# Grouped-query attention on one core: part of the exponentials as linear pieces on VectorE, row tiles one head apart, and a planned instruction order

## The chip, the cores and the metric

One core of a Trainium2 chip. The metric is device time in microseconds (us) of one execution. Executions come with a state: a run more than 1.5% above the fastest of the same kernel counts as slow, and only fast runs are compared.

## The reference

Batch 8, 8 query heads, 2 key/value heads, 1024 positions, 64 columns per head, all float32. Cut to what matters:

```python
q, k, v = (np.random.randn(8, n, 1024, 64).astype(np.float32) * 0.1 for n in (8, 2, 2))

for g in range(n_kv_heads):                       # 2 groups of 4 query heads
    scores = scale * np.matmul(q_group, k_group.transpose(0, 1, 3, 2))   # scale = 1/8
    attn = np.exp(scores - scores.max(axis=-1, keepdims=True))
    attn = attn / (attn.sum(axis=-1, keepdims=True) + 1e-08)
    output[:, q_start:q_end] = np.matmul(attn, v_group)
```

With these inputs a score has a standard deviation of about 0.01 (64 products of size 0.01, times 1/8), so every weight is within a few per cent of every other.

## The kernel before

A *cell* is one score block: 128 keys x 512 queries of one head. There are 1024 of them. Head 0 of a pair lives in the upper 64 rows of TensorE (row tile 0), head 1 in the lower 64 (row tile 1). ScalarE takes the exp of three cells at once (1536 columns):

```python
nc.tensor.matmul(                                  # L125: one score cell
    state["tile"][:, len(state["cells"]), :],
    lhsT=kT[b][side * D : (side + 1) * D, c * 128 : (c + 1) * 128],
    rhs=qT[(b, j)][side * D : (side + 1) * D, qb * QBS : (qb + 1) * QBS],
    start=True, stop=True)
...
nc.scalar.activation(out=pt[:, 0 : len(cells), :],  # L105
    in_=state["tile"][:, 0 : len(cells), :], func=AF.Exp, scale=scale)
```

The output product of a cell is eight small matmuls, four blocks of 128 queries times two halves of the 128 keys; each half uses one row tile and 65 columns of `v` (the last column is ones and gives the sum). Both row tiles add into the same output bank, one after the other, and a no-op on the Sync queue, the *turn*, hands the bank over:

```python
mm = nc.tensor.matmul(                              # L148
    ops[:, side, qs * (D + 1) : (qs + 1) * (D + 1)],
    lhsT=pcell[(u * NKC + c, side)][lo : lo + 64, qs * 128 : (qs + 1) * 128],
    rhs=vt[(b, side)][lo : lo + 64, c, :], ...)
...
turn[0] = nc.sync.nop().ins                         # L162
tc.add_manual_dep(turn[0], last.ins.name, SYNC, reason="bank")
```

The same Sync queue carries the DMA transposes that bring `q` and `k` in, forty of them, each of all 1024 rows:

```python
nc.gpsimd.dma_start(out=qscr..., in_=q[b, j::NPAIR]...)   # cast to 16 bit through DRAM
nc.sync.dma_start_transpose(out=qt, in_=qscr)             # L81
```

The softmax here doesn't subtract the row's maximum and nothing guards it: scores larger than these inputs give would overflow.

Of the kernel before, what the change touches and what calls it, by code (L numbers as in the profile page):

```python
# [7 lines left out]


@with_exitstack  # L10
def kernel(
    ctx: ExitStack,
    tc: tile.TileContext,
    q: bass.AP,
    k: bass.AP,
    v: bass.AP,
    out: bass.AP,
):
    nc = tc.nc
    FP32 = mybir.dt.float32  # L20
    BF16 = mybir.dt.bfloat16
    AF = mybir.ActivationFunctionType
    ALU = mybir.AluOpType

    B, H, S, D = q.shape
    G = k.shape[1]
    NPAIR = H // G
    NKC = S // 128
    QBS = 512
    NQB = S // QBS  # L30
    NQS = QBS // 128
    scale = 1.0 / math.sqrt(D)




    units = [(b, j, qb) for b in range(B) for j in range(NPAIR) for qb in range(NQB)]
    NSTEP = len(units) * NKC
    LAG = NKC + 2
    WIDTHS = (3, 3)  # L40

    scr_pool = ctx.enter_context(
        tc.tile_pool(name="scr", bufs=2, space=bass.MemoryType.DRAM)
    )
    qT_pool = ctx.enter_context(tc.tile_pool(name="qTpool", bufs=2 * NPAIR))
    kT_pool = ctx.enter_context(tc.tile_pool(name="kTpool", bufs=2))
    v_pool = ctx.enter_context(tc.tile_pool(name="vpool", bufs=3 * G))
    p_pool = ctx.enter_context(tc.tile_pool(name="ppool", bufs=12))
    ostage_pool = ctx.enter_context(tc.tile_pool(name="ostage", bufs=3))
    recip_pool = ctx.enter_context(tc.tile_pool(name="recip", bufs=3))  # L50
    spools = [
        ctx.enter_context(
            tc.tile_pool(name=f"spsum{w}", bufs=1, space=bass.MemoryType.PSUM)
        )
        for w in range(len(WIDTHS))
    ]
    opool = ctx.enter_context(
        tc.tile_pool(name="opsum", bufs=1, space=bass.MemoryType.PSUM)
    )

    qT = {}
    kT = {}
    vt = {}

    def load_batch(b):
        kscr = scr_pool.tile([S, G * D], BF16, name="kscr")
        nc.gpsimd.dma_start(  # L67
            out=kscr.rearrange("s (g d) -> s g d", g=G),
            in_=k[b].rearrange("g s d -> s g d"),
        )  # L70
        kt = kT_pool.tile([128, S], BF16, name="kT")
        nc.sync.dma_start_transpose(out=kt, in_=kscr)  # L72
        kT[b] = kt
        for j in range(NPAIR):
            qscr = scr_pool.tile([S, G * D], BF16, name=f"qscr{j}")
            nc.gpsimd.dma_start(  # L76
                out=qscr.rearrange("s (g d) -> s g d", g=G),
                in_=q[b, j::NPAIR].rearrange("g s d -> s g d"),
            )
            qt = qT_pool.tile([128, S], BF16, name="qT")  # L80
            nc.sync.dma_start_transpose(out=qt, in_=qscr)  # L81
            qT[(b, j)] = qt
        for g in range(G):
            vs = v_pool.tile([128, NKC, D + 1], BF16, name="vs")
            nc.gpsimd.memset(vs[:, :, D], 1.0)  # L85
            nc.gpsimd.dma_start(  # L86
                out=vs[:, :, 0:D],
                in_=v[b, g].rearrange("(c p) d -> p c d", p=128),
            )
            vt[(b, g)] = vs  # L90

    pcell = {}
    ops_of = {}
    turn = [None]
    SYNC = mybir.DependencyInfo(
        mybir.DependencyClass.Sync, mybir.DependencyReason.DATA
    )
    state = {"tile": None, "cells": [], "n": 0}

    def flush():  # L100
        cells = state["cells"]
        if not cells:
            return
        pt = p_pool.tile([128, max(WIDTHS), QBS], BF16, name="pt")
        nc.scalar.activation(  # L105
            out=pt[:, 0 : len(cells), :],
            in_=state["tile"][:, 0 : len(cells), :],
            func=AF.Exp,
            scale=scale,
        )  # L110
        for slot, key in enumerate(cells):
            pcell[key] = pt[:, slot, :]
        state["tile"] = None
        state["cells"] = []
        state["n"] += 1

    def score_step(i):
        b, j, qb = units[i // NKC]
        c = i % NKC
        full = False  # L120
        for side in range(G):
            w = state["n"] % len(WIDTHS)
            if state["tile"] is None:
                state["tile"] = spools[w].tile([128, WIDTHS[w], QBS], FP32, name=f"sps{w}")
            nc.tensor.matmul(  # L125
                state["tile"][:, len(state["cells"]), :],
                lhsT=kT[b][side * D : (side + 1) * D, c * 128 : (c + 1) * 128],
                rhs=qT[(b, j)][side * D : (side + 1) * D, qb * QBS : (qb + 1) * QBS],
                start=True,
                stop=True,  # L130
            )
            state["cells"].append((i, side))
            if len(state["cells"]) == WIDTHS[w]:
                flush()

    def output_step(i):
        u, step = divmod(i, NKC)
        b, j, qb = units[u]
        half, part = divmod(step, NKC // 2)
        if step == 0:  # L140
            ops_of[u] = opool.tile([128, G, 512], FP32, name="ops")
        ops = ops_of[u]
        for c in (2 * part, 2 * part + 1):
            for qs in range(NQS):
                for rows in range(2):
                    side = rows ^ half
                    lo = rows * 64
                    mm = nc.tensor.matmul(  # L148
                        ops[:, side, qs * (D + 1) : (qs + 1) * (D + 1)],
                        lhsT=pcell[(u * NKC + c, side)][  # L150
                            lo : lo + 64, qs * 128 : (qs + 1) * 128
                        ],
                        rhs=vt[(b, side)][lo : lo + 64, c, :],
                        start=(half == 0 and c == 0 and qs == 0),
                        stop=(half == 1 and c == NKC - 1 and qs == NQS - 1),
                    )
                    if half == 1 and c == 0 and qs == 0:

                        tc.add_manual_dep(mm.ins, turn[0].name, SYNC, reason="bank")
                    last = mm  # L160
        if step == NKC // 2 - 1:
            turn[0] = nc.sync.nop().ins  # L162
            tc.add_manual_dep(turn[0], last.ins.name, SYNC, reason="bank")
        if step < NKC - 1:
            return
        for c in range(NKC):
            for side in range(G):
                del pcell[(u * NKC + c, side)]
        o = ops_of.pop(u)[:, :, 0 : NQS * (D + 1)].rearrange(
            "p g (s e) -> p g s e", e=D + 1  # L170
        )
        rec = recip_pool.tile([128, G, NQS], FP32, name="rec")
        nc.vector.reciprocal(out=rec, in_=o[:, :, :, D])  # L173
        ost = ostage_pool.tile([128, G, NQS, D], FP32, name="ost")
        nc.vector.tensor_tensor(  # L175
            out=ost,
            in0=o[:, :, :, 0:D],
            in1=rec.unsqueeze(3).to_broadcast([128, G, NQS, D]),
            op=ALU.mult,
        )  # L180
        for side in range(G):
            nc.sync.dma_start(
                out=out[b, j + side * NPAIR].rearrange("(s p) d -> p s d", p=128)[
                    :, qb * NQS : (qb + 1) * NQS, :
                ],
                in_=ost[:, side],
            )

    per_batch = NPAIR * NQB * NKC
    with tc.manual_schedule():  # L190
        load_batch(0)
        for i in range(NSTEP + LAG):
            if i < NSTEP:
                if i % per_batch == 4 and i // per_batch + 1 < B:
                    load_batch(i // per_batch + 1)
                score_step(i)
                if i == NSTEP - 1:
                    flush()
            if i >= LAG:
                output_step(i - LAG)  # L200


# [28 lines left out]
```

## Time and profile before

| | before |
|---|---|
| median time (4 runs) | 545.56 us (544.34 to 547.38) |
| ScalarE busy | 466.6 us, 86% |
| TensorE matmuls | 9216 (1024 scores, 8192 outputs) |
| VectorE busy | 57.5 us, 11% |
| DMA transposes on Sync | 40 |

The rows that carry the bound are in the prediction below.

The view of all instructions of one line, for the transposes: minimum, median and maximum duration in ns, then the first and the last start.

```profile
L81 SPq DMA_TRANSPOSE qT<-qscr x32: 1162/1247/3865, 9.5 to 421.4; - x32
```

A transpose of 1024 rows holds the Sync queue 1.25 us.

### The profile page before, as it was taken

The page shows a single profiled execution, that of the slowest core. Times are in us where ns is not written, and L with a number is a line of the kernel's source. Part 1 is how long each engine was busy: PE and PEld are TensorE (multiplying, and loading weights), DVE is VectorE, ACT ScalarE, POOL GpSimd, SP SyncE. Part 2 cuts the span into 40 slices and gives each one's busy share as a digit, 9 for nine tenths or more (in the row PEclk, how much of TensorE's full clock was granted, in tenths as well). Part 3 has the DMA queues: queue, kind, packets, megabytes, share of the DMA engines.
Part 4 walks back from the last instruction along what each step waited for, and adds up shares of the span by engine and source line. Part 5 has one row for each costly group of instructions (what it writes and reads, how often), then busy time and mean ns, then how long its engine had stood idle before and what let it go on. Part 6 is the DMA issues. An engine that isn't in the chain of part 4 may idle for free.

```text
span 545.4 us, 19767 instructions
## 1 busy us (share of the span) xinstructions
PE 357.6 (66%) x9216; PEld 228.7 (42%) x9216; DVE 57.5 (11%) x128; ACT 466.6 (86%) x343; POOL 98.2 (18%) x76
## 2 busy tenths in 40 slices
PE   0436766676748767587775767767674867767764
PEld 0024443444435444354443444444442544444443
DVE  0001011011101101011110110101110110111101
ACT  0547999699978999699996999959997899999994
POOL 8986100440007100080002600010000000000000
PEclk9988999699996999889996999869999699899999
DMA  9999923891159911698117921371114211111012
GB/s 75 156 149 157 157 45 69 114 132 40 32 111 97 97 41 43 117 115 83 40 33 127 132 47 41 68 109 41 41 37 99 45 39 41 41 42 40 22 41 61
DMA packets 209107, 41.13 MB, mean 75 GB/s; under 512 B 209024, under 2 KB 209024, under 8 KB 209024
## 3 DMA queue, kind: packets, MB, share of 16 engines
q0 software_dynamic: 99200, 12.59, 36.3%
q1 hardware_dynamic: 109824, 27.28, 26.0%
q8 instruction: 72, 1.18, 0.9%
q14 instruction: 11, 0.09, 0.1%
HBM read 25.17 MB, written 27.26 MB: 96 GB/s over the span
## 4 chain that ended last, share of the span: by engine, by line
ACT 45%; PE 21%; issue 13%; DVE 7%; SPq 7%; DMA 4%; POOL 3%; ACTq 0%; POOLq 0%
ACT pt L105 45%; PE ops L148 12%; PE sps L125 9%; SPq L81 6%; DVE ost L175 5%; DMA qscr<-in_q_dram 4%; POOL qscr L76 2%; DVE rec L173 2%; POOL kscr L67 1%; SPq L72 0%; POOL vs L86 0%; ACTq L105 0%; POOL vs L85 0%; SPq L162 0%; POOLq L215 0%
## 5 line engine op out<-in xcount | busy, mean ns | idle before, releaser
L105 ACT ACTIVATE pt<-sps 128x1536 bf16<-128x1536 f32 x342 | 465.3, 1472 | 70.8 <-PE sps L125 70.6
L125 PE MATMUL sps<-qT,kT 64*128 64x512 bf16 x1024 | 282.7, 410 | 121.4 <-ACT pt L105 99.8
L148 PEld LDWEIGHTS <-pt 64*128 64x128 bf16 x8192 | 217.0, 98 | 225.7 <-issue 83.8
L148 PE MATMUL ops<-vs,pt 64*128 64x65 bf16 x8192 | 260.0, 197 | 61.9 <-SPq L162 36.1
L125 PEld LDWEIGHTS <-kT 64*128 64x128 bf16 x1024 | 79.4, 99 | 86.4 <-issue 70.5
L76 POOL DMA_DIRECT2D qscr<-in_q_dram x32 | 72.0, 4055 | 3.8 <-DMA kscr<-in_k_dram 1.8
L173 DVE RECIPROCAL rec<-ops 128x8 f32<-128x8 f32 x64 | 13.3, 208 | 482.1 <-PE ops L148 482.1
L85 POOL MEMSET vs<- 128x8 bf16 x16 | 13.3, 833 | 251.3 <-PE ops L148 251.3
L175 DVE TENSOR_TENSOR ost<-ops,rec 128x512 f32<-128x512 f32 x64 | 44.2, 691 | 2.2
L67 POOL DMA_DIRECT2D kscr<-in_k_dram x8 | 16.5, 2058 | 0.9 <-POOLq L215 0.9
L86 POOL DMA_DIRECT2D vs<-in_v_dram x16 | 14.4, 897 | 9.6 <-POOL vs L85 5.9
L105 ACT ACT_TABLE_LOAD x1 | 1.3, 1283 | 0.7 <-PEq L215 0.7
L215 POOL MEMSET const-float32-0.0<- 128x1 f32 x1 | 0.1, 98 | 0.2 <-issue 0.2
L215 POOL MEMSET const-float32-1.0<- 128x1 f32 x1 | 0.1, 98 | 0.0
L215 POOL MEMSET const-bfloat16-1.0<- 128x1 bf16 x1 | 0.1, 98 | 0.0
L215 POOL MEMSET const-uint8-127<- 128x1 uint8 x1 | 0.1, 98 | 0.0
## 6 DMA issues: line engine op xcount, KB each, us to landing
out_dram<-ost SPq DMA_DIRECT2D x128, 128.0 KB, 2.2
qscr<-in_q_dram POOLq DMA_DIRECT2D x32, 256.0 KB, 12.6
kscr<-in_k_dram POOLq DMA_DIRECT2D x8, 256.0 KB, 6.2
vs<-in_v_dram POOLq DMA_DIRECT2D x16, 128.0 KB, 5.3
qT<-qscr SPq DMA_TRANSPOSE x32, 3.8
kT<-kscr SPq DMA_TRANSPOSE x8, 3.7
```

The lines of the kernel that those rows point to most:

```text
L67: nc.gpsimd.dma_start(out=kscr.rearrange("s (g d) -> s g d", g=G), in_=k[b].rearrange("g s d -> s g d"),)
L76: nc.gpsimd.dma_start(out=qscr.rearrange("s (g d) -> s g d", g=G), in_=q[b, j::NPAIR].rearrange("g s d -> s g d"),)
L81: nc.sync.dma_start_transpose(out=qt, in_=qscr)
L85: nc.gpsimd.memset(vs[:, :, D], 1.0)
L86: nc.gpsimd.dma_start(out=vs[:, :, 0:D], in_=v[b, g].rearrange("(c p) d -> p c d", p=128),)
L105: nc.scalar.activation(out=pt[:, 0 : len(cells), :], in_=state["tile"][:, 0 : len(cells), :], func=AF.Exp, scale=scale,)
L125: nc.tensor.matmul(state["tile"][:, len(state["cells"]), :], lhsT=kT[b][side * D : (side + 1) * D, c * 128 : (c + 1) * 128], rhs=qT[(b, j) ...
L148: mm = nc.tensor.matmul(ops[:, side, qs * (D + 1) : (qs + 1) * (D + 1)], lhsT=pcell[(u * NKC + c, side)][lo : lo + 64, qs * 128 : (qs + 1) ...
L173: nc.vector.reciprocal(out=rec, in_=o[:, :, :, D])
L175: nc.vector.tensor_tensor(out=ost, in0=o[:, :, :, 0:D], in1=rec.unsqueeze(3).to_broadcast([128, G, NQS, D]), op=ALU.mult,)
L215: nc = _bacc.Bacc("TRN2", target_bir_lowering=False, num_devices=1)
```

## The change

The intent: ScalarE is the bound, VectorE is nearly idle. So about a quarter of the cells (250 of 1024) get their exp on VectorE. The bits of a 16-bit float, read as an integer, are a piecewise linear logarithm, so `a*x + b` written as an unsigned integer and read as a float is a piecewise linear exp with one piece per octave. Adding it up four times, with the bits moved by 0, 32, 64 and 96 and the `v` rows weighted by 2^(-w/4) to undo the move, gives four pieces per octave. TensorE does the adding: such a cell costs 32 output matmuls in place of 8. The order of all instructions is worked out in advance by a simulated plan with assumed durations; row tile 1 runs one head behind row tile 0; transposes are cut into four pieces of 256 rows. The diff, cut to its core:

```diff
+KNOT_W = (1.0, 0.83984375, 0.70703125, 0.59375)
+KNOT_BITS = (0, 32, 64, 96)
+def make_plan(nu, nkc, nk):
+    QK, MM, EXP, P1, ADD, NORM = 0.216, 0.0295, 0.925, 0.665, 0.155, 0.64
+    FROM_PE, FROM_ACT, FROM_DVE, TURN = 0.28, 0.18, 0.12, 0.45
+    LIVE_A, LIVE_D, PENDING, OMAX, DMAX, SKEW = 26, 5, 8, 3, 1, 2
...                                    # picks, step by step, what can start first
+    PIECE = 256
...
+    def transpose(key, dst, n):                                   # L274
+        rows = slice(n * PIECE, (n + 1) * PIECE)
+        nc.sync.dma_start_transpose(out=dst[:, rows], in_=scratch[key][rows, :])
...
+    def weigh_v(b, g):                                            # L298
+        for w in range(NK):
+            nc.gpsimd.tensor_scalar(out=vs[:, g, w, :, 0:D], in0=vf, scalar1=KNOT_W[w], ...)
...
+    def exps(n, cells):                          # L361, now two cells, 1024 columns
+        nc.scalar.activation(out=pt[:, 0:m], in_=psum.pop(("A", n))[:, 0:m], func=AF.Exp, scale=scale)
+    def knot_bits(cell, n, g, slot):                              # L371
+        nc.vector.tensor_scalar(out=pd[:, 0, slot], in0=psum.pop(cell),
+            scalar1=bits_scale, scalar2=bits_bias, op0=ALU.mult, op1=ALU.add)
+    def move_knots(g, m):                                         # L384
+        for w in range(1, NK):
+            nc.vector.tensor_scalar(out=pd[:, w, 0:m], in0=pd[:, 0, 0:m],
+                scalar1=float(KNOT_BITS[w]), scalar2=None, op0=ALU.add)
+    def output_mm(r, s, cell, w, qs, opens, enters, closes, bk):  # L399
+        mm = nc.tensor.matmul(ops_of[s][:, qs * E1 : (qs + 1) * E1],
+            lhsT=p_of[cell][w][rows, qs * 128 : (qs + 1) * 128],
+            rhs=vsets[b % VSETS][rows, side, w, c, :], start=opens, stop=closes)
+    def turn(s):                                                  # L412
+        turn_of[s] = nc.sync.nop().ins
...
+            at(t0 - 22.0, cast, ("k", b), k[b])
+            for n in range(S // PIECE):
+                at(t0 - 10.0 + 0.7 * n, transpose_k, b, n)
```

In the profiles of the changed kernel L350 is the score matmul, L361 the exp, L371 the linear piece, L384 the moves, L399 the output matmul, L412 the turn, L274 the transposes, L289 the load of `v`, L298 its weighing, L428 the output store.

## The prediction

The forecast came to 13 + 380 + 3 + 10 + 4 = 410 us. Its 380 was taken between a sum of 390 for VectorE and 366 with overlap. Of the 390 the 250 pieces (173 us) are left; the terms of the 189 moves, of the 128 normalisations and of the casts and copy at the start, 217 us in all, are cut. In the trace after, these three were busy for 149.4, 77.0 and 2.1 us. The third rival, at 425 us (VectorE held up by GpSimd's work), is cut too, with a part of the reason given for the 10 us, and so is one reason each for and against the first rival. The 35 ns of overlap and the "some 3 us" of cast, transpose and copy were guesses; in the trace after, VectorE's 698 instructions overlapped by 32 us, 45 ns each, and the cast, transposes and copy of the first q took 2.8 us (from 7.06 to 9.88 us).

> **What bounds the kernel now.** I read the page first: busy shares, then the forty slices, then the chain.
>
> ```profile
> PE 357.6 (66%) x9216; PEld 228.7 (42%) x9216; DVE 57.5 (11%) x128; ACT 466.6 (86%) x343; POOL 98.2 (18%) x76
> ...
> ACT  0547999699978999699996999959997899999994
> ...
> PEclk9988999699996999889996999869999699899999
> ...
> ACT 45%; PE 21%; issue 13%; DVE 7%; SPq 7%; DMA 4%; POOL 3%; ACTq 0%; POOLq 0%
> ```
>
> ScalarE is the bound: busy 466.6 of 545.4 us, 9 in most slices. VectorE is nearly free. The ACT row has dips to 4-7 at a regular distance, and the clock row dips with it: these are batch boundaries. Then the groups kept apart by form:
>
> ```profile
> L105 ACT ACTIVATE pt<-sps 128x1536 bf16<-128x1536 f32 x341 | 464.8, 1475 | 70.8 <-PE sps L125 70.6
> L105 ACT ACTIVATE pt<-sps 128x512 bf16<-128x512 f32 x1 | 0.6, 616 | 0.0
> L175 DVE TENSOR_TENSOR ost<-ops,rec 128x512 f32<-128x512 f32 x64 | 44.2, 691 | 2.2
> L173 DVE RECIPROCAL rec<-ops 128x8 f32<-128x8 f32 x64 | 13.3, 208 | 482.1 <-PE ops L148 482.1
> ```
>
> The two forms of the exp give the slope: (1475 - 616) / 1024 = 0.839 ns per column. ScalarE is idle for 545.4 - 466.6 = 79 us. The timeline says where. First the start and one boundary:
>
> ```profile
> 19.41 9.51 ACT L105 ACTIVATE pt<-sps 128x1536 bf16<-128x1536 f32 x7 [17.39 <-PE sps L125]
> ...
> 44.40 2.79 ACT L105 ACTIVATE pt<-sps 128x1536 bf16<-128x1536 f32 x2 [10.85 <-PE sps L125]
> ```
> ```profile
> 159.09 3.92 SPq L81 DMA_TRANSPOSE qT<-qscr  x3
> 163.12 0.46 PEld L148 LDWEIGHTS <-pt 64*128 64x128 bf16 x16 [4.82 <-SPq L162]
> ...
> 165.13 2.79 ACT L105 ACTIVATE pt<-sps 128x1536 bf16<-128x1536 f32 x2 [4.72 <-PE sps L125]
> ```
>
> At 163 us TensorE waits 4.8 us for L162, the "turn" through the Sync queue that hands a bank from one row tile to the other. The turn stands behind transposes in that queue, which wait for casts. ScalarE starves with it. So the idle time is about 19 us of start, 7 of tail (the last exp ends at 538.1) and 53 in between, mostly seven boundaries. The saturated stretch gives TensorE's own rates:
>
> ```profile
> 176.10 0.42 PE L148 MATMUL ops<-vs,pt 64*128 64x65 bf16 x16 [0.81 <-DVE ost L175]
> 176.35 0.38 PE L125 MATMUL sps<-qT,kT 64*128 64x512 bf16 x2
> 176.57 0.40 PE L148 MATMUL ops<-vs,pt 64*128 64x65 bf16 x16
> 176.81 0.70 PE L125 MATMUL sps<-qT,kT 64*128 64x512 bf16 x2
> ```
>
> A pair of score matmuls, one per row tile, takes 176.57 - 176.35 = 0.22 us; sixteen output matmuls take 176.81 - 176.57 = 0.24 us, 15 ns each with both row tiles at work.
>
> [...] the pitch here is 1.337 us ((5.48 - 1.475) / 3 in a run of four that lasts 5.48 us), so the overlap is 0.14.
> [...]
> [...]
> [...] The trace shows score pairs overlapping; scores of one row tile beside outputs of the other is not something it settles.
>
> **The change part by part.** The counts come from the instruction order of the two programs.
>
> ScalarE: 342 exps of 1536 columns become 387 of 1024; 250 of the 1024 score cells go to VectorE. Duration by the slope: 1475 - 512 x 0.839 = 1045 ns; pitch 1.337 - 0.430 = 0.908 us. 387 x 0.908 = 351 us, against 342 x 1.337 = 457. Off the bound: 106 us.
>
> VectorE gains: 250 linear pieces (128x512, fp32 PSUM to 16 bit), at the 691 ns of the eviction row 173 us. 189 knot moves, nearly all 128x2048 16-bit in SBUF[...]. 128 normalisations in place of 64, half as wide: 0.24 us from reciprocal to multiply (175.11 to 175.35 in the timeline)[...]. [...] Sum 390 us. If neighbours overlap by about 35 ns, as ScalarE's do by more, 695 operations give back 24: 366. I take 380. So VectorE, at 57.5 us today, becomes the longest engine, a little above ScalarE.
>
> TensorE: 1024 score matmuls stay (512 x 0.22 = 113 us). The 774 ScalarE cells cost 8 output matmuls each, the 250 VectorE cells 32 (four knots): 6192 + 8000 = 14192 instead of 8192, at 15 ns 213 us. Sum 326 us: below the other two, but at about 80% use; today it is (113 + 123) = 236.
>
> Boundaries: casts are issued about 15 planned microseconds ahead of the transposes that need them, transposes are cut in four (the whole one holds the Sync queue 1.25 us), so a turn should stand behind about 0.3-0.5 us at most. Output banks are one per head, up to three at a time, so the 0.8 us wait for the multiply seen above goes. Nearly all of the 53 us should go.
>
> Start: batch 0's first k and q come by plain loads and TensorE transposes, no cast. Four 256 KB loads at up to 157 GB/s (the best slice) are 6.7 us, with 2.2 us of landing (the output transfers' median) and cast, transpose and copy of some 3 us: first exp near 13 us instead of 19.4. Against it: the next q casts stand on GpSimd behind eight weighings of v that wait for v; the second pair's q may be late by some 3 us.
>
> Sum: 13 (start) + 380 (VectorE) + 3 (second pair) + 10 (waits among three nearly full engines, about 2.5%[...]) + 4 (last output transfer and end) = 410 us, 0.75 of today.
>
> **Rivals.**
> First, TensorE becomes the bound. Many scores now stand alone among outputs of the other row tile (653 single ones in the order). If a score holds up the other tile, 1024 x 0.22 + 213 is 438, and the span about 460. Against: [...]the order puts seven or eight output matmuls of the other tile behind a single score, just a score's length. [...]
> Second, the plan slips (the order was computed from assumed durations, which I do not use). Three engines stand at 80-95%, with two exp tiles, four other banks and strict queues; a late result in one queue delays the next. If that costs 8% rather than 2.5%, 432 us.
> [...]
> Fourth, VectorE's operations overlap well and ScalarE's 351 us bounds with it: 13 + 366 + 10 = 390.
> Fifth, the turn still sticks in the Sync queue, which now carries 128 turns and 152 transposes: at 0.4 us each a sixth of the time is covered; 128 turns x 1/6 x 0.2 is 4 us, not decisive.
>
> **Range and chances.** The fourth gives the low edge, 392. The first three give 425-455, each with less than even chance; I put the high edge at 436. ScalarE loses over 100 us for certain and VectorE would have to cost 45% more than worked out to bring the time back to 534, so faster by over 2%: 0.96.
>
> **What would show it.** Right: ScalarE 387 exps of about 1045 ns; VectorE busy 360-390 us with pieces near 690[...]; TensorE waits on L162-like turns small; granted clock 1.0 without boundary dips; first exp near 13 us. Wrong: [...] TensorE busy without gaps while both others wait would be the first rival; ScalarE dips at boundaries would mean that casts are still late.

## More of the kernel before

```profile
q8 instruction: 72, 1.18, 0.9%
```

The instructions have a DMA queue of their own. 1.18 MB in 72 packets is 16 KB each, and 72 packets for 9216 pairs of a weight load and a matmul is 2 x 9216 / 72 = 256 instructions a packet.

## The result, and the profile after

| | before | after |
|---|---|---|
| median time (4 runs each) | 545.56 us | 589.18 us (586.88 to 593.32) |
| span of the profiled run | 545.4 us | 591.5 us |
| mean granted TensorE clock, profiled run | 0.927 | 0.885 |

A ratio in this document is the mean time of one kernel's fast runs over the mean of the other's fast runs of the same rounds, so not quite the ratio of the medians. Here it is 1.0805, with a 95% interval of 1.0736 to 1.0874. The change made the kernel 8% slower; the prediction said 25% faster.

From the page of the changed kernel: busy time and instructions; busy tenths of ScalarE and the granted clock in forty slices; the instruction queue; and the chain of work that ended last, by engine.

```profile
PE 438.4 (74%) x15232; PEld 382.2 (65%) x15232; DVE 379.0 (64%) x698; ACT 378.7 (64%) x389; POOL 182.9 (31%) x120
...
ACT  4358467875658465765687765666755765587860
...
PEclk9669879998889888887889988888898877799997
...
q8 instruction: 119, 1.95, 1.5%
...
PE 49%; SPq 25%; DVE 9%; issue 9%; DMA 3%; ACT 3%; POOL 2%; ACTq 0%
```

Before, ScalarE showed 9 in most slices and the chain ran through it. Now no engine shows 9 anywhere for long: ScalarE and VectorE are busy 379 us each, almost exactly what was predicted, and they are idle for the other 212. A quarter of the chain stands at SPq, the Sync queue, which here carries transfers and turns. The groups say that the work itself was sized well:

```profile
L361 ACT ACTIVATE pa<-aps 128x1024 bf16<-128x1024 f32 x387 | 376.4, 1025 | 187.8 <-PE aps L350 173.7
...
L371 DVE TENSOR_SCALAR pd<-bank 128x512 uint16<-128x512 f32 x250 | 169.0, 686 | 135.2 <-PE bank L350 133.3
L298 POOL TENSOR_SCALAR vset<-vstage 128x512 bf16<-128x512 f32 x64 | 104.3, 1630 | 328.5 <-DMA vstage<-in_v_dram 276.3
L384 DVE TENSOR_SCALAR pd<-pd 128x2048 uint16<-128x2048 uint16 (+1 forms) x189 | 149.4, 847 | 0.5
```

Exps 1025 ns (1045 predicted), pieces 686 (691), moves 847 (the median is 689). The last column is the reading: ScalarE and VectorE both sit idle for lack of scores, L350, 174 and 133 us. So they starve, and TensorE, which feeds them, is what has to be looked at. From the view of waits of the changed kernel (what waited, for whom, us in total, times, longest):

```profile
PEld L399 <- SPq L412: 92.6, 49, 4.9
PE bank L399 <- SPq L412: 83.2, 45, 4.8
...
PEld L399 <- issue: 55.2, 94, 3.2
PE bank L399 <- issue: 31.5, 44, 3.1
```

Two waits of TensorE. The first is for turns, 83 us in 45 waits. The second, "issue", is time in which it waited for nothing that the profile shows, 31 us. One stretch of the timeline of the Sync queue (start, length, instruction):

```profile
197.88 2.31 SPq L274 DMA_TRANSPOSE qT<-scr  x1
200.31 1.14 SPq L289 DMA_DIRECT2D vstage<-in_v_dram  x2
201.50 3.86 SPq L274 DMA_TRANSPOSE qT<-scr  x2
```

and TensorE's weight loads in the same stretch:

```profile
200.41 0.15 PEld L399 LDWEIGHTS <-pa 64*128 64x128 bf16 x3 [0.91 <-issue]
205.47 0.10 PEld L399 LDWEIGHTS <-pa 64*128 64x128 bf16 x1 [4.91 <-SPq L412]
```

A turn that TensorE needs at 200.6 us stands in the Sync queue behind a load and two transposes, and comes out at 205.4, when the last of them lets go. The view of stretches shows what that does to everybody (TensorE, its loads, VectorE, ScalarE, GpSimd busy, then the granted clock):

```profile
200.00:205.00 5.00, 0.28 (x4) 0.15 (x3) 0.23 (x1) 0.87 (x1) 0.36 (x1) 0.83 0.60 134
205.00:210.00 5.00, 4.53 (x108) 4.25 (x109) 1.31 (x3) 2.01 (x2) 4.76 (x4) 0.50 0.18 42
```

Five microseconds in which no engine does as much as 1 us of work, then five at half the clock in which TensorE gets through 108 matmuls. And the line of the transposes, after:

```profile
L274 SPq DMA_TRANSPOSE qT<-scr x124: 1105/1230/2664, 27.3 to 555.1; - x124
```

Beside the line shown of before, a transpose of 256 rows holds the queue as long as one of 1024: 1230 against 1247 ns. So 152 in place of 40 hold it 3.6 times as long: summed over all records of `q` and `k`, the Sync queue was inside transposes for 217.9 us of 591.5 after, and for 60.7 of 545.4 before.

### The profile page after: what moved, and what is told of

The parts are those of the page before. It is cut to its first block, busy times and chain, and to the rows that moved or that the text cites. A ratio compares the mean times of both kernels' runs of the same rounds, so it can differ in the third digit from the quotient of the medians.

```text
span 591.5 us, 32803 instructions
## 1 busy us (share of the span) xinstructions
PE 438.4 (74%) x15232; PEld 382.2 (65%) x15232; DVE 379.0 (64%) x698; ACT 378.7 (64%) x389; POOL 182.9 (31%) x120
## 4 chain that ended last, share of the span: by engine, by line
PE 49%; SPq 25%; DVE 9%; issue 9%; DMA 3%; ACT 3%; POOL 2%; ACTq 0%
PE bank L399 39%; SPq L274 20%; PE aps L350 8%; DVE pd L384 4%; SPq L428 3%; ACT pa L361 3%; PE bank L350 2%; DVE pd L371 2%; POOL vset L298 2%; DVE ost L422 1%; SPq L289 1%; DMA qT<-scr 1%; DMA scr<-in_q_dram 1%; DVE rec L420 1%; DMA vstage<-in_v_dram 1%
## 5 line engine op out<-in xcount | busy, mean ns | idle before, releaser
L361 ACT ACTIVATE pa<-aps 128x1024 bf16<-128x1024 f32 x387 | 376.4, 1025 | 187.8 <-PE aps L350 173.7
L399 PE MATMUL bank<-vset,pa 64*128 64x65 bf16 x6192 | 265.1, 198 | 84.4 <-SPq L412 70.6
L399 PE MATMUL bank<-vset,pd 64*128 64x65 bf16 x8000 | 292.7, 199 | 33.1 <-issue 17.9
L399 PEld LDWEIGHTS <-pa 64*128 64x128 bf16 x6192 | 228.3, 99 | 123.9 <-SPq L412 78.3
L399 PEld LDWEIGHTS <-pd 64*128 64x128 bf16 x8000 | 259.5, 100 | 45.5 <-issue 25.4
L371 DVE TENSOR_SCALAR pd<-bank 128x512 uint16<-128x512 f32 x250 | 169.0, 686 | 135.2 <-PE bank L350 133.3
L350 PE MATMUL aps<-qT,kT 64*128 64x512 bf16 x774 | 222.8, 416 | 24.5 <-DMA qT<-scr 15.1
L298 POOL TENSOR_SCALAR vset<-vstage 128x512 bf16<-128x512 f32 x64 | 104.3, 1630 | 328.5 <-DMA vstage<-in_v_dram 276.3
L384 DVE TENSOR_SCALAR pd<-pd 128x2048 uint16<-128x2048 uint16 (+1 forms) x189 | 149.4, 847 | 0.5
L350 PE MATMUL bank<-qT,kT 64*128 64x512 bf16 x250 | 104.4, 424 | 0.6 <-DVE ost L422 0.6
L350 PEld LDWEIGHTS <-kT 64*128 64x128 bf16 x1024 | 85.6, 98 | 29.0 <-DMA qT<-scr 14.9
L420 DVE RECIPROCAL rec<-bank 128x4 f32<-128x4 f32 x128 | 22.7, 178 | 63.3 <-PE bank L399 62.8
```

Source lines behind the costliest of these rows:

```text
L298: nc.gpsimd.tensor_scalar(out=vs[:, g, w, :, 0:D], in0=vf, scalar1=KNOT_W[w], scalar2=None, op0=ALU.mult,)
L350: nc.tensor.matmul(dst, lhsT=kT[b][rows, c * 128 : (c + 1) * 128], rhs=qT[(b, j)][rows, qb * QBS : (qb + 1) * QBS], start=True, stop=True,)
L361: nc.scalar.activation(out=pt[:, 0:m], in_=psum.pop(("A", n))[:, 0:m], func=AF.Exp, scale=scale)
L371: nc.vector.tensor_scalar(out=pd[:, 0, slot], in0=psum.pop(cell), scalar1=bits_scale, scalar2=bits_bias, op0=ALU.mult, op1=ALU.add,)
L384: nc.vector.tensor_scalar(out=pd[:, w, 0:m], in0=pd[:, 0, 0:m], scalar1=float(KNOT_BITS[w]), scalar2=None, op0=ALU.add,)
L399: mm = nc.tensor.matmul(ops_of[s][:, qs * E1 : (qs + 1) * E1], lhsT=p_of[cell][w][rows, qs * 128 : (qs + 1) * 128], rhs=vsets[b % VSETS][r ...
```

## The experiments

The first theory was the queue: turns stand behind transposes, and cutting each transpose in four made that worse. Its rivals at first were the plan (an order made from assumed durations slips and stalls), and TensorE itself, slower than the 15 ns that I had assumed. As runs came in, the latter split into *array* theories (matmuls of one shape hold up those of another) and theory *F*: TensorE's instructions arrive in blocks of 256, and a block takes a fixed time to arrive, whatever is in it (m1_stream below: 3.46 us from block to block with 65 columns and with 17). Kernels were run, each beside the kernel before on the same chip:

| run | what it is | median us | ratio to before, 95% interval |
|---|---|---|---|
| e1_whole | after, transposes whole again | 531.11 | 0.971 (0.968 to 0.975) |
| e2_half | after, transposes in halves | 534.44 | 0.978 (0.972 to 0.984) |
| e3_notr | after, only batch 0 transposed | 515.91 | 0.945 (0.941 to 0.950) |
| e4_turnact | after, turn through ScalarE's queue | 534.64 | 0.967 (0.963 to 0.971) |
| m1_stream | matmuls alone | 386.17 | one look, state unknown |
| e5_fullrow | e1, 128-row outputs, no turn | 597.76 | no interval |
| e6_narrow | e1, 17 columns in place of 65 | 533.80 | 0.975 (0.969 to 0.980) |
| e7_two | e1, two pieces per octave | 434.99 | 0.794 (0.790 to 0.798) |
| e8_skip | e1, half of the knots' matmuls left out | 464.26 | 0.849 (0.846 to 0.851) |
| e9_start | e7, one cast earlier | 436.30 | 0.796 (0.792 to 0.800) |
| e10_two256 | e7, transposes in quarters | 531.01 | 0.970 (0.966 to 0.975) |
| e11_plan | e1, no cell on VectorE | 573.07 | 1.037 (1.029 to 1.045) |
| e12_replan | e7, plan with measured durations | 445.69 | 0.814 (0.811 to 0.818) |
| e13_one | e7, one piece per octave | 394.02 | 0.721 (0.717 to 0.724) |
| e14_turn2 | e7, turn through ScalarE's queue | 428.40 | 0.784 (0.781 to 0.788) |
| e15_both | e12 and e14 together | 442.59 | 0.807 (0.802 to 0.813) |
| e16_one_act | e13, turn through ScalarE's queue | 389.87 | 0.714 (0.710 to 0.719) |
| e17_one_g1 | e16, cells not grouped | 386.71 | 0.704 (0.701 to 0.706) |

The kernel before ran at 546.2 to 547.1 us. A median here is over all four runs of a kernel; the ratio uses the fast ones alone. Ten of these kernels had slow runs among the four: two each in e4, e5 and e11, one each in e6, e7, e8, e9, e12, e15 and e17.

**What "correct" can say here.** All runs matched the reference but m1_stream, e6_narrow and e8_skip. But e3_notr uses batch 0's `q` and `k` for all batches: with scores of about 0.01 every output is nearly the mean of `v`. So the check sees a wrong sum or a wrong weight, not a rough exp. Where a version has fewer pieces, it is less exact.

### The queue

**e1_whole**

```diff
-    PIECE = 256
+    PIECE = 1024
```

> Transposes of 1024 rows in one piece: 38 instead of 152. Theory A (a transpose holds the Sync queue about 1.2 us whatever its size, the turns stand behind it, TensorE stalls and its clock halves): Sync queue time of transposes falls from 218 to about 60 us, TensorE's waits for the turn from 83 to about 30 us, time to 440-500. Rival B (the plan slips anyway, in three nearly full engines): 560-600. Rival C[...]: 570-600, since nothing of it is changed.

531.11 us, 58 us less than after. The transposes' line, and TensorE's waits, of this run:

```profile
L274 SPq DMA_TRANSPOSE qT<-scr x31: 1159/1210/2287, 27.5 to 489.3; - x31
```
```profile
PE bank L399 <- issue: 64.7, 74, 3.8
...
PE bank L399 <- SPq L412: 4.8, 6, 2.4
```

Whole transposes take 1.21 us each, the same as quarters. The wait for turns falls from 83.2 to 4.8 us. One constant, which I had counted as an improvement, cost 58 us. That rules out B (the plan) and C (VectorE held up by GpSimd's work; what a trace shows of that is in the last part) as the whole cause (560 or more), but it also misses theory A's 440 to 500 us: the kernel is now only 3% faster than before, and the wait "issue" has doubled.

**e2_half**

```diff
-    PIECE = 1024
+    PIECE = 512
```

> Transposes of 512 rows: 76. Theory A: between the whole ones and the quarters, 490-545. B and C: 560-600.

534.44 us: inside what was expected, but hardly above e1 although there are twice as many transposes. Its waits show why:

```profile
PE bank L399 <- issue: 44.9, 60, 2.2
...
PE bank L399 <- SPq L412: 24.9, 24, 3.2
```

24.9 us of turns, 20 more than e1, and 20 less of "issue". The two together are 69.8 us here, 69.5 in e1 and 83.2 + 31.5 = 114.7 after. Waiting for a turn costs nothing here as long as it lies beside whatever "issue" is. After, it no longer fits: 45 us more waiting, 58 us more time. So there is a second limit under the first.

**e4_turnact**

```diff
     def turn(s):
-        turn_of[s] = nc.sync.nop().ins
+        turn_of[s] = nc.scalar.nop().ins
```

> The turn goes through ScalarE's queue instead of Sync; the 152 transposes stay. Theory A: TensorE no longer waits for Sync; 430-500, if ScalarE's queue hands the turn on within a microsecond. If the transposes hurt through late data (q or k not there) rather than through the turn: above 550, with TensorE waiting for qT. B and C: 560-600.

Transposes in quarters again, 152 of them, but the turn no longer behind them. The fast runs took 528.2 and 529.0 us (two more, 540 and 541). No wait for a Sync turn is left, and TensorE's longest wait is "issue" with 65.5 us. This undoes the same loss as e1 by another way and with all the transposes still there: it was the turn behind them, not the transposes' own lateness. It is a miss against the 430 to 500 us expected, for the reason that e1 and e2 show: something else holds TensorE.

**e3_notr** (wrong: batches 1 to 7 use batch 0's `q` and `k`)

```diff
     def transpose_k(b, n):
+        if b > 0:
+            kT[b] = kT[0]
+            return
...
     def transpose_q(b, j, n):
+        if b > 0:
+            qT[(b, j)] = qT[(0, j)]
+            return
```

> Wrong result on purpose: batches 1 to 7 use the transposed q and k of batch 0, so that 12 transposes are left; casts and all else stay. Theory A: 410-450, turn waits under 15 us, clock near 1.0 after the start. B and C: 550-590.

515.91 us: a clear miss. With nearly all transposes gone the queue theory allowed 410 to 450 us. So the queue is worth 58 us to quarters and at most 15 more, and the rest of the gap to 410 has another cause. The trace of this run gave the first hint. I numbered TensorE's instructions (loads, matmuls and the few waits in its queue) and looked where more than 0.25 us passed from one start to the next: of 154 such pauses, 83 lay at the same place in blocks of 256 instructions, and those 83 made up 73.3 us. Counted alike, the place is the same in other runs: 48 pauses there (45.3 us) after, 92 (92.5 us) in e1, one (0.3 us) before.

### The block of 256

**m1_stream** (wrong: matmuls on constants, no attention). Six stretches of back-to-back matmuls that wait for nothing:

```python
for i in range(2048):                  # L39: two row tiles in turn, 65 columns
    r = i % 2
    rows = slice(64 * r, 64 * r + 64)
    nc.tensor.matmul(y[r][:, 0:65], lhsT=w[rows], rhs=x[rows, 0:65], start=True, stop=True)
# then the same with 17 columns (L43), 130, 260; then 128 rows with 65 and 130 columns
```

> Wrong result on purpose: TensorE alone, streams of matmuls with their weight loads, no waits and no transfers: 2048 of 64 rows and 65 columns on alternating row tiles, then 1536 of 17, 1536 of 130, 1024 of 260 columns, then 1536 of 128 rows and 65 columns and 1536 of 128 rows and 130 columns. Theory F (TensorE's instructions come from memory in blocks of 256, one block per about 3.4 us at best, and 128 matmuls with their loads fill a block): 65 and 17 columns both at 26-27 ns per matmul, with a stall at each 256th instruction; from 260 columns on no stall. Theory A alone (array work of 15 ns per matmul): 65 columns at 15-16 ns, 17 columns no slower, no periodic stall.

The timeline of the weight loads, 65 columns, and then 17:

```profile
10.50 2.00 PEld L39 LDWEIGHTS <-w 64*128 64x128 bf16 x128 [1.13 <-issue]
13.96 2.00 PEld L39 LDWEIGHTS <-w 64*128 64x128 bf16 x128 [1.45 <-issue]
17.41 2.00 PEld L39 LDWEIGHTS <-w 64*128 64x128 bf16 x128 [1.45 <-issue]
```
```profile
61.05 1.75 PEld L43 LDWEIGHTS <-w 64*128 64x128 bf16 x128 [1.97 <-issue]
64.51 1.79 PEld L43 LDWEIGHTS <-w 64*128 64x128 bf16 x128 [1.71 <-issue]
```

This is the clearest picture. 128 loads with their matmuls, 256 instructions, run off in 2.00 us: 15.6 ns a matmul, my 15 ns. Then TensorE stands for 1.45 us with nothing to wait for that the profile shows. The pitch is 13.96 - 10.50 = 3.46 us, 27 ns a matmul. With a quarter of the columns the pitch is again 64.51 - 61.05 = 3.46 us: between these two it does not depend on the work. (The first stretch ran at full clock, 1.00 granted, the second at half, 0.50; a block of 17 columns ran off in 1.75 to 1.79 us, so TensorE stood idle after each block in both.) Other blocks came up to 4.00 us apart; the mean pitch is 3.60 us in either stretch, 28 ns a matmul. Over whole stretches, 65 columns took 56.4 us for 2048 (27.5 ns each) and 17 columns 43.5 us for 1536 (28.3 ns). Where 128 matmuls last longer than that, the pauses vanish: 130 columns 29.8 ns, 260 columns 55 ns, 128 rows with 65 columns 30.3 ns (single matmuls, start to start).

The packets of the instruction queue agree: no two of them are less than 3.25 us apart in any run (the shortest interval is 3.25 to 3.42 us in all but e5, 3.87, and e11, 4.70), and the median is 3.65 in e3, 4.03 after, and 6.62 before. So the kernel before met this limit only now and then, and the changed kernel lives near it: 119 blocks take 411 us at 3.45 us and 428 us at the mean pitch of 3.60, before any wait that can't lie beside the fetching.

Before, little of this shows (6.62 us a block, one pause at the block's place); in m1_stream's small matmuls TensorE stood for 1.1 to 2.2 us between the blocks looked at. That the pause is the wait for the block is inferred from the packets and the pitch; no record of the profile names it.

**e6_narrow** (wrong: 17 of the 65 columns, on e1)

```diff
-            ops_of[s][:, qs * E1 : (qs + 1) * E1],
+            ops_of[s][:, (qs + 1) * E1 - 17 : (qs + 1) * E1],
...
-            rhs=vsets[b % VSETS][rows, side, w, c, :],
+            rhs=vsets[b % VSETS][rows, side, w, c, E1 - 17 :],
...
```

> Wrong result on purpose, on top of the whole transposes: output matmuls write 17 columns in place of 65, so TensorE's array has less to do, its instructions are as many. F: within 2% of the whole transposes' 531. If TensorE's array work bounds: 480 or less.

533.80 us against e1's 531.11: no gain, as F expected. But this run says less than it seems to. Its granted clock was only 0.57 to 0.65, and the profile is of a slow run. And a quarter of the columns is not a quarter of the time: where that profile is at full clock, output matmuls on different row tiles start 15 ns apart at the median in place of e1's 16, and on the same one 26 in place of 29 (the trace does not name the tiles; they are taken from the program's order). So fewer columns gain nothing; that blocks are what limits is carried by m1_stream and e8.

**e5_fullrow** (on e1: outputs of row tile 0 left out, those of row tile 1 made 128 rows high, no turn needed)

```diff
+        if r == 0:
+            return
...
-        rows = slice(r * 64, (r + 1) * 64)
+        rows = slice(0, 128)
...
```

> On top of the whole transposes: the two 64-row output matmuls of a cell become one of 128 rows, so 7096 in place of 14192 and no turn; 16240 TensorE instructions in place of 30464. F: the stalls at each 256th instruction go, time 440-480 if a 128-row pair of load and matmul takes under 45 ns; above that TensorE's array binds. Slip theory B: no gain, 520 or more.

The 45 ns there are an estimate (7096 x 0.045 + 113 = 432 us); m1_stream had such a pair every 30.3 ns. This halves the output matmuls (63 blocks in place of 119), so F alone allowed far less than 531 us. It took 592 and 593 us in its fast runs. Its timeline shows what I had not thought of:

```profile
322.87 0.39 PE L350 MATMUL aps<-qT,kT 64*128 64x512 bf16 x1
323.18 0.27 PEld L401 LDWEIGHTS <-pd 128*128 128x128 bf16 x7 [0.23 <-issue]
323.19 0.39 PE L401 MATMUL bank<-vset,pd 128*128 128x65 bf16 x7
```

From a score of 64 rows to the first output of 128 rows 323.19 - 322.87 = 0.32 us pass, against 0.22 for a whole *pair* of scores in the prediction's timeline. It is so throughout this run: 557 outputs that follow a score at full clock start 319 ns after it at the median. The two heights do not run side by side here, and 591 of the 1024 scores are followed by an output. TensorE is 92% busy, packets come 8.5 us apart at the median, so F does not bind here and this run says nothing against it. It is a different bound: in this order, full height next to half-height scores costs more than half of the instructions saves.

**e8_skip** (wrong: on e1, VectorE computes all four knots, TensorE adds up only two)

```diff
             _, _, r, s, cell, terms, opens, enters, closes, bk, mm = op
+            terms = min(terms, 2)
```

> Not the reference's sum on purpose, on top of the whole transposes with four pieces: TensorE adds only two of the four pieces of each VectorE cell, so 10192 output matmuls and 22432 TensorE instructions (88 blocks in place of 119); VectorE's and ScalarE's work and the planned order stay. F: 430-470, and stalls at the 256th instruction fall from about 104 us to under 45. If the gain of the two-piece version came from VectorE's and ScalarE's smaller loads: 510-530.

464.26 us, 67 less than e1, inside what F expected. This is the cleanest test: ScalarE's and VectorE's instructions are all there (VectorE is busy 383.8 us, 380.0 in e1), the plan is the same, the queue is the same; only 4000 of 15232 matmuls are gone. By the time alone it would not tell fetching from TensorE's own work, since fewer matmuls are also less to run. The pauses tell it: those at the block's place fall from 92 in e1 (92.5 us) to 11 (11.4 us). TensorE's time outside of pauses falls from 373 to 339 us, and pauses elsewhere rise from 63 to 112 us, so much of what was saved is lost again to other waits.

**e7_two** (on e1)

```diff
-KNOT_W = (1.0, 0.83984375, 0.70703125, 0.59375)
-KNOT_BITS = (0, 32, 64, 96)
-KNOT_SHIFT = -2.056524609695944
+KNOT_W = (1.0, 0.70703125)
+KNOT_BITS = (0, 64)
+KNOT_SHIFT = -1.057455691487803
```

> On top of the whole transposes: two linear pieces per octave in place of four; the plan then gives VectorE 306 cells, and 10640 output matmuls remain: 23328 TensorE instructions, 91 blocks in place of 119. F: 119 - 91 = 28 blocks of 3.4 us are 95 us of fetching less, time 440-475. B: about 510-530, since three engines stay full. The result is a little less exact, within tolerance.

434.99 us, a little below what was expected: a VectorE cell now costs 16 matmuls in place of 32 and one move per group in place of three, so the plan sends 306 cells there, and there are 91 blocks. With 91 x 3.60 = 328 us the blocks leave room on the average, though 44 pauses (42.9 us) still lie at their place. Two pieces ripple by 0.75% either way where four ripple by 0.19% (by arithmetic, not by a run).

**e10_two256** (e7 with transposes in quarters)

```diff
-    PIECE = 1024
+    PIECE = 256
```

> The two-piece version, but with the transposes in quarters as in the changed kernel: 152 of them, about 218 us of the Sync queue in place of 52. Theory A: the turns wait again, 475-505. If the Sync queue only hurt together with the fetch stalls: 435-445.

531.01 us, 96 more than e7 and more than was expected. Here the block limit doesn't cover for the turns: TensorE waits 99.7 us for turns and 11.8 for "issue". The same slow queue costs more where less else lies beside its waits.

### The plan, the start and the clock

**e11_plan** (e1 with no cell for VectorE)

```diff
-    LIVE_A, LIVE_D, PENDING, OMAX, DMAX, SKEW = 26, 5, 8, 3, 1, 2
+    LIVE_A, LIVE_D, PENDING, OMAX, DMAX, SKEW = 26, 5, 8, 3, 0, 2
```

> No cell to VectorE: the planned order with row tile 1 one head behind and whole transposes alone, 512 exps of 1024 columns, 8192 output matmuls, 72 blocks of instructions. ScalarE 512 x 0.973 = 498 us, plus 13 of start and about 10 of waits: 515-535, against 546 of before. F has no part in it (72 x 3.4 = 245 us); B (the plan slips) would make it 550 or more.

A miss: 562.9 and 570.1 us in the fast runs, slower than before with the same 9216 scores and outputs (and 16 transposes at the start) and 72 blocks. ScalarE has more to do than before, 484.6 us busy against 466.6, since it takes two cells at once and not three. That is 18 of the 20 us lost (566.5 against 546.6 by the fast runs), so the new order, apart from this, neither gains nor loses much. The stretches tell when it loses (the first columns as above; ScalarE is the fourth, the clock the sixth):

```profile
40.00:60.00 20.00, 14.42 (x371) 11.10 (x369) 3.03 (x10) 19.72 (x23) 0.00 (x0) 1.00 0.26 55
...
160.00:180.00 20.00, 16.43 (x352) 13.38 (x352) 2.43 (x8) 17.20 (x20) 0.00 (x0) 0.76 0.19 42
```

Early on ScalarE is full, 19.72 of 20 us, at full clock. Later the clock drops to 0.76 and ScalarE starves at 17.20, with fewer matmuls on TensorE (352 against 371). Through the run TensorE spent 196 us at half clock, in 52 episodes of 3.4 us and more. After the start, the 7.5 us before an episode had no gap between matmul starts longer than 0.9 us, and the 3.4 us before it held 30 to 51 matmuls, so TensorE was not idle. The other stretches of that length at full clock held 63 matmuls at the median, against 34 just before an episode. So thin work went before the half clock in this run; what exactly sets it is not settled by these runs.

**e9_start** (e7, with the cast of the second pair's `q` ahead of the weighings)

```diff
         load_v(0)
+        cast(("q", 0, 1), q[0, 1::NPAIR])
         for g in range(G):
             weigh_v(0, g)
...                                    # and the planned cast of this q is left out
```

> On top of the two-piece version with whole transposes (435): the cast of the second pair's q goes ahead of the eight weighings of v at the start. TensorE waits 8 us there for that q now; expected 425-430. If the q is not what the start waits for: 435.

436.30 us, no gain. ScalarE did go on at 22.7 us in place of 30.8 in e7, but the 8 us were lost again later. Perhaps the planned order has slack after a late start that it otherwise lacks; no run shows it.

**e12_replan** (e7, the plan given measured durations and a charge for instruction blocks)

```diff
-    QK, MM, EXP, P1, ADD, NORM = 0.216, 0.0295, 0.925, 0.665, 0.155, 0.64
+    QK, MM, EXP, P1, ADD, NORM = 0.216, 0.0295, 0.95, 0.685, 0.21, 0.64
+    FETCH, BURST, fetched = 0.0135, 3.4, 0.0
...
+            fetched = max(fetched, t - BURST) + words * FETCH
+            issue = max(t, fetched)
```

> Two pieces, whole transposes, the order planned anew with durations as measured (exp 0.95, piece 0.685, move 0.21 per cell) and a charge of 13.5 ns per TensorE instruction after a burst of one block. If what is left above 410 comes from an order that doesn't know of the fetch: 405-425. If not: 430-440.

445.69 us, 2.5% slower than e7 where a gain was expected. A plan that is truer in its averages was not better; why, I did not find out.

**e14_turn2** and **e15_both** (e7 and e12, with the turn through ScalarE's queue)

```diff
-        turn_of[s] = nc.sync.nop().ins
+        turn_of[s] = nc.scalar.nop().ins
```

> Two pieces, whole transposes, the turn through ScalarE's queue. TensorE waits 13-17 us for turns in Sync's; if that is all of what Sync still costs: 420-428. If ScalarE's queue holds turns as long: 435.

> The new plan and the turn through ScalarE's queue together: 395-415 if both gain by themselves; no better than the better of the two otherwise.

428.40 us for e14, at the edge of what was expected, and 442.59 for e15. So even with whole transposes the turns in the Sync queue are worth some 5 us (428.3 against 433.8 by the fast runs), and the new plan loses with either queue. e14 is the best version with two pieces.

### Fewer instructions still

**e13_one** (e7 with one piece per octave: no moves at all, no extra matmuls)

```diff
-KNOT_W = (1.0, 0.70703125)
-KNOT_BITS = (0, 64)
-KNOT_SHIFT = -1.057455691487803
+KNOT_W = (1.0,)
+KNOT_BITS = (0,)
+KNOT_SHIFT = -0.05753274588835121
```

> One piece per octave (less exact), whole transposes: 342 VectorE cells and 8192 output matmuls by the plan, 72 blocks of TensorE instructions, no knot moves. F says that blocks matter only while they are the longest: 119 blocks gave 531, 91 gave 435; 72 blocks are 248 us of fetching, below ScalarE's 341 exps x 0.97 = 331 us, so from 91 to 72 the time falls less than 28 blocks did: 385-425. If every block cost 3.4 us still: 370. If fetching were not what bound: no lower than 430.

394.02 us, with 342 cells on VectorE and 72 blocks, as many as before. **e16_one_act** puts the turn on ScalarE's queue as above, **e17_one_g1** stops grouping four cells, which without moves serves no purpose:

```diff
-GROUP = 4
+GROUP = 1
...
-    pd_pool = ctx.enter_context(tc.tile_pool(name="pdpool", bufs=5))
+    pd_pool = ctx.enter_context(tc.tile_pool(name="pdpool", bufs=20))
```

(and the plan's limit `LIVE_D` from 5 to 20).

> One piece per octave, whole transposes, the turn through ScalarE's queue: the two gains together, 394 less the 7 that the turn gave with two pieces: 384-392.

> The same, and a VectorE cell is ready at once in place of in groups of four (with one piece there are no knot moves to share): 375-390; no change if nothing waited for the groups.

389.87 and 386.71 us, both inside what was expected. (From e13 to e16 the intervals of the ratio overlap, so that the turn gains here too is not clear of noise.) Busy times of e17:

```profile
PE 317.8 (82%) x9232; PEld 250.5 (65%) x9232; DVE 288.4 (75%) x597; ACT 325.4 (84%) x345; POOL 101.9 (26%) x63
```

With 9232 matmuls in place of 15232, ScalarE is at 84% again. This is the fastest version, 0.704 of before, and beats both kernels. Its price: one linear piece per octave ripples by about 3% either way, and as said above, inputs of this size can't show whether that is enough. It would have to be checked with scores of a few units before anybody used it.

## Why the prediction was wrong, point by point

**The bound and the work were read right.** ScalarE did bound before; it lost work as worked out, though each exp took 376.4 / 387 = 0.973 us of busy time where the pitch was put at 0.908 (back to back it was 0.918: ten exps in 9.29 us, below). VectorE's busy time came out at 379.0 us for 380 predicted, and this hides two errors that cancel: longer moves, and neighbours that overlapped by 32 us in all, where 380 allowed 10. The 189 moves took 847 ns at the mean. The 138 that lie beside no weighing and no cast of GpSimd took 681 ns on average, at most 696. The 38 beside a weighing took 1097, the 13 others beside the issue of a cast 1869. Together that is 31 us of longer moves, on an engine that was idle for 212. No engine's busy time explains 589 us.

**First failed step, in "Boundaries":** "transposes are cut in four (the whole one holds the Sync queue 1.25 us), so a turn should stand behind about 0.3-0.5 us at most". A quarter was taken to cost a quarter. It costs 1.23 us, like a whole one, and four came in a row. The same number then went into the fifth rival, which named the right wait: "128 turns x 1/6 x 0.2 is 4 us, not decisive". Measured, the queue was covered by transposes for 217.9 / 591.5 = 0.37 of the time rather than 1/6, and a waiting turn stood for 83.2 / 45 = 1.85 us rather than 0.2: 83 us. Both factors of a product carried the same error. Worth: 58 us (after against e1), 96 us where nothing else covers it (e10 against e7). "Nearly all of the 53 us should go" did not happen; they were replaced by more.

**Second failed step, in "TensorE":** "14192 instead of 8192, at 15 ns 213 us. Sum 326 us: below the other two". The 15 ns came from sixteen matmuls in one 0.24 us stretch of before. It is a true rate, and m1_stream shows it again (15.6 ns), but only inside a block of 256 instructions, and only where row tiles alternate from matmul to matmul, as they do in both of these programs. Sustained, the stream of m1_stream is 27 to 28 ns and counts instructions, scores and loads included: 119 blocks x 3.45 us = 411 us, above both other engines. And in the changed program 38% of neighbouring output matmuls are on the same row tile. In e1 at full clock these start 29 ns apart at the median, those on different tiles 16, all together 21 ns at the mean (the tiles again from the program's order). So in e1 TensorE ran for 373 us outside of its pauses, where 326 was predicted, and stood for 92.5 us more at the block's place. No rival named either. The first rival came closest: TensorE did become the bound, but not as it said, by scores that hold up the other row tile. In e1, of 790 scores at full clock that an output follows, the output started 22.5 ns later at the median, and only in 19% of the cases as late as 150 ns. What e8 took away of TensorE's instructions was worth 67 us (against e1, with 87 blocks left).

**Third, the clock.** The prediction wanted a "granted clock 1.0 without boundary dips". In the changed kernel TensorE ran at half clock for 138 us in all, 82 before and 59 in e1. The excess over e1, 79 us, goes when the transposes are whole, so it comes with the stalls on turns, as at 205 us above, and is part of the first 58 us rather than beside it. How much the remaining episodes cost was not measured.

**Fourth, the start.** The first exp came at 10.58 us (13 predicted), better. But "the second pair's q may be late by some 3 us" was 15.5. ScalarE's and GpSimd's timelines of the changed kernel:

```profile
10.58 9.29 ACT L361 ACTIVATE pa<-aps 128x1024 bf16<-128x1024 f32 x10 [0.70 <-PE aps L350]
35.40 1.94 ACT L361 ACTIVATE pa<-aps 128x1024 bf16<-128x1024 f32 x2 [15.52 <-PE aps L350]
```
```profile
7.44 14.27 POOL L298 TENSOR_SCALAR vset<-vstage 128x512 bf16<-128x512 f32 x8 [5.49 <-DMA vstage<-in_v_dram]
```

The cast stands behind eight weighings that take 14.3 us together. By e9, removing part of that gained nothing in the end.

**The sum.** 589 less 58 (turns, e1) is 531; less 67 (blocks, e8) is 464. The 54 us that are left over 410 lie among the same-tile matmuls (e8 runs 339 us outside of pauses), 11.4 us of block pauses, the half clock, longer moves beside GpSimd's work (31 us in the changed kernel), 17.7 us of turns that e8 still waits for, and the plan's slips. They were not separated further, and the plan's part is the least understood (e11, e12). Two sums of the prediction are off without changing this: (5.48 - 1.475) / 3 is 1.335, not 1.337; and VectorE would have to cost (534 - 410) / 380 = 33% more, not 45%, to bring the time back to 534.

**What was right in mechanism:** taking exps to VectorE does pay. With two pieces and the turn out of the Sync queue it runs at 428 us, with one piece at 387. The predicted 410 was for four pieces, and with four pieces no run came below 464, even with matmuls left out.

## What to carry to other kernels

A rate read from sixteen instructions is a peak, not a rate (here 15 ns against 27 to 28 sustained): before multiplying it by fourteen thousand, ask whether the order that gave it still holds, look for what comes in larger units, and count instructions as well as work. Before you cut a transfer into pieces, ask what of its cost is per piece (here 1230 ns for 256 rows, 1247 for 1024), and what else stands in that queue; a no-op that hands over a buffer belongs in a queue that carries nothing slow (e4, with all 152 transposes: 528 and 529 us in place of 589). When one wait is taken away and the time moves little, compare the sums of waits: here the turns and the pauses stood in for each other, and only their total told what a change was worth.
